# Attention scores whose two matmuls both take 128 rows: each half of q stands twice in SBUF and meets the high and low part of k

## The chip, the cores and the metric

The kernel runs on one core of a Trainium2 chip. The metric is the device time of one execution in microseconds (us). Engines are named as the profile names them: PE is TensorE's matmul stream, PEld its weight loads, DVE VectorE, ACT ScalarE, POOL GpSimd, and SP the engine from whose queue most transfers are issued.

## The reference, cut to what matters

One layer of a bidirectional encoder: a projection, two kinds of attention, an output projection with a LayerNorm, and a mixture of single-neuron experts (PEER). The scores of both attentions are products over a head dimension of 64:

```python
HEAD_DIM = 64
h = x @ w_in[l]                                        # 1024 tokens
# group A: 8 heads, 2 kv heads, blocks of 128 queries against 3 blocks of keys
s = jnp.einsum('bnqkgd,bnskd->bnkgqs', qb, kw).astype(jnp.float32) * (HEAD_DIM ** -0.5)
# group B: 8 heads, a window of 8 rows by 16 columns of the token grid
s = jnp.einsum('brqhd,brikhd->brhqik', qg, kr).astype(jnp.float32) * (HEAD_DIM ** -0.5)
...
x = layer_norm(ALPHA * x + mixed, ln1_g[l], ln1_b[l])
x = layer_norm(ALPHA * x + peer(x, peer_wq[l], peer_keys[l], peer_u[l], peer_v[l]), ln2_g[l], ln2_b[l])
```

## The kernel before

The kernel works in full float32 precision from a narrower matmul type: an operand is split into a high part and a low part (`split`, line 85: ACT rounds, DVE takes the rest), and the product is the sum of high by high, high by low and low by high, in one PSUM accumulation.

The program has three parts. **Projection and first attention** (to about 310 us of the trace): `project(0)` and `project(1)` multiply the input's halves of 512 tokens by 18 column groups of `w_in`, in the order of the table `PORD`. Groups 0 to 7 give q, 8 to 12 give k, 13 to 17 give v. The split q and k go to DRAM tiles `qd` and `kd` through POOL's queue, from two-buffer tiles `sh` (high) and `sl` (low): for each group of q three stores, high, low and high again, so that `qd` holds for each head 64 rows of high, 64 of high once more and 64 of low. For each group of k two stores, high and low. **Attention and routing** (to about 1156 us): for each of 8 blocks of 128 tokens `att_steps(t)` computes group A, then group B. `att_out` follows for each pair of blocks (line 486), then `route`, which picks the experts (lines 558 to 565, `top16` and `decode` on DVE), scatters gate values from POOL (line 165), and `build`, which writes dense gate matrices for three blocks (lines 605 to 620). **Experts** (to the end): the dense half on PE (`hstage`, `vres`, `vflush`) with gathers on POOL and DVE beside it.

The order of the instructions on each engine is made by the framework's scheduler, which interleaves these steps by its own model of their durations; each engine then takes its instructions strictly in that order.

A score is made in `scores` (line 381): `kk` holds a head's keys, 64 rows of high and 64 of low. The first matmul has as weights `qq`, 128 rows (high q twice), and meets all of `kk`. The second has `ql`, 64 rows (low q), and meets the high 64 rows of `kk` alone. Both write one PSUM tile `ps` (two buffers). DVE then adds the bias, takes the row maximum and moves the score to SBUF in one instruction (lines 408 for A, 455 for B). There are 24 such pairs in a block of tokens, 192 in all, of 256, 288 or 384 columns. `load_q` fetches `qq` and `ql` for four heads with one transfer each from SP's queue, 32 times.

Of the kernel before, what the change touches and what calls it, by code (L numbers as in the profile page):

```python
# [11 lines left out]
F32 = mybir.dt.float32  # L12
F32R = mybir.dt.float32r
# [8 lines left out]
P = 128  # L22
S = 1024
# [34 lines left out]
def trunk(ctx, tc, x, xt, wqk, wo, gn, sink, biasa, biasb, ln, wq, keyst, uv, ut, vt, out):  # L58
    nc = tc.nc
    f = lambda ap: ap.bitcast(F32)  # L60
# [24 lines left out]
    def split(hi, lo, raw, lo_eng=None):  # L85
        cp = nc.scalar.copy(hi, raw)  # L86
        nc.vector.tensor_sub(lo, raw, f(hi))  # L87
        return cp

    def mm3(ps, wh, wl, mh, ml, first, last):  # L90
        nc.tensor.matmul(ps, wh, mh, start=first, stop=False)  # L91
        nc.tensor.matmul(ps, wh, ml, start=False, stop=False)  # L92
        nc.tensor.matmul(ps, wl, mh, start=False, stop=last)  # L93
# [10 lines left out]
        nc.vector.scalar_tensor_tensor(tmp, r, mv[:, 0:1], lnt[:, 0, :], op0=OP.subtract, op1=OP.mult)  # L104
        nc.vector.scalar_tensor_tensor(dst, tmp, rs[:, 0:1], lnt[:, 1, :], op0=OP.mult, op1=OP.add)

    qd = tc.dram_tile([16, 3, 64, S], F32, name="qd")
    kd = tc.dram_tile([10, 2, 64, S], F32, name="kd")
    xs = tc.dram_tile([NT, P, D], F32, name="xs")
    wqd = tc.dram_tile([16, 2, P, KT, P], F32, name="wqd")  # L110
# [129 lines left out]
    with ExitStack() as att:  # L240
# [3 lines left out]
        qp = att.enter_context(tc.tile_pool(name="qp", bufs=2))  # L244
# [18 lines left out]
        def load_w(src):  # L263
            raw = wp.tile([P, KT, P], F32, name="wraw", bufs=WB)
            nc.sync.dma_start(raw, src)
            hi = wp.tile([P, KT, P], F32R, name="whi", bufs=WB)
            lo = wp.tile([P, KT, P], F32R, name="wlo", bufs=WB)
            split(hi, lo, raw)
            return hi, lo

        def project(half):
            o = half * 512
            ts = slice(4 * half, 4 * half + 4)
            xs_ = []
            first = load_w(wqk[PORD[0]])
            for k in range(KT):
                raw = wp.tile([P, 512], F32, name="xraw", bufs=5)
                (nc.scalar if half == 0 and k % 2 else nc.sync).dma_start(raw, xt[:, k, o:o + 512])
                xh = xp.tile([P, 512], F32R, name=f"xh{k}")
                xl = xp.tile([P, 512], F32R, name=f"xl{k}")  # L280
                split(xh, xl, raw)
                xs_.append((xh, xl))
            for n, c in enumerate(PORD):
                hi, lo = first if n == 0 else load_w(wqk[c])
                ps = pp.tile([P, 512], F32, name="pq", bufs=2)
                for k, (xh, xl) in enumerate(xs_):
                    mm3(ps, hi[:, k, :], lo[:, k, :], xh, xl, k == 0, k == KT - 1)
                if c < 13:
                    sh = wp.tile([P, 512], F32R, name="sh")
                    sl = wp.tile([P, 512], F32R, name="sl")  # L290
                    if c < 8:
                        sc = wp.tile([P, 512], F32, name="qo")
                        nc.scalar.activation(sc, ps, AF.Copy, scale=0.125)
                    else:
                        sc = ps
                    last = split(sh, sl, sc)
                    for i, m in ((0, sh), (2 if c < 8 else 1, sl)):
                        if c < 4:
                            g0 = 4 * (c // 2) + c % 2
                            dst = qd[g0:g0 + 3:2, i, :, o:o + 512]  # L300
                        elif c < 8:
                            dst = qd[2 * c:2 * c + 2, i, :, o:o + 512]
                        else:
                            dst = kd[2 * (c - 8):2 * (c - 8) + 2, i, :, o:o + 512]
                        nc.gpsimd.dma_start(dst, f(m))
                    if c < 8:
                        nc.gpsimd.dma_start(qd[g0:g0 + 3:2, 1, :, o:o + 512] if c < 4 else qd[2 * c:2 * c + 2, 1, :, o:o + 512], f(sh))
                else:
                    va = wp.tile([P, 512], F32, name="qo")
                    last = nc.scalar.copy(va, ps)  # L310
                    pt = pp.tile([P, 4, P], F32, name="pv")
                    for j in range(4):
                        nc.tensor.transpose(pt[:, j, :], va[:, j * P:(j + 1) * P], ident)
                    nc.vector.tensor_copy(v[:, ts, (c - 13) * P:(c - 12) * P], pt)
# [50 lines left out]
        def att_steps(t):  # L365
            tok = slice(t * P, (t + 1) * P)

            def load_q(grp):
                qq = qp.tile([P, 4, P], F32R, name="qq")
                ql = qp.tile([64, 4, P], F32R, name="ql")  # L370
                grp = qd[4 * grp:4 * grp + 4, :, :, tok].rearrange("h i p n -> (i p) h n")
                nc.sync.dma_start(f(qq), grp[0:P])
                nc.sync.dma_start(f(ql), grp[P:])
                return qq, ql

            def load_k(hd, k0, n):
                kk = kp.tile([P, 576], F32R, name="kk")
                nc.sync.dma_start(f(kk[:, :n]), kd[hd, :, :, k0:k0 + n].rearrange("i p n -> (i p) n"))
                return kk

            def scores(ps, q, i, kk, cols):
                qq, ql = q
                nc.tensor.matmul(ps, qq[:, i, :], kk[:, cols], start=True, stop=False)
                nc.tensor.matmul(ps, ql[:, i, :], kk[0:64, cols], start=False, stop=True)

            blocks = [m for m in (t - 1, t, t + 1) if 0 <= m < NT]
            n = P * len(blocks)
# [8 lines left out]
            for hb in range(2):  # L396
                ss = {}
                q = load_q(hb)
                for i in (2 * hb, 2 * hb + 1):
                    for g in range(2):  # L400
                        ps = ps_s.tile([P, 512], F32, name="ps")
                        scores(ps[:, :n], q, 2 * g + i - 2 * hb, ka[g], slice(0, n))
                        h = 4 * g + i
# [11 lines left out]
                sl = lambda a: hv(a)[:, :, i0:i0 + 2]  # L415
# [13 lines left out]
            if t < 2 or t > 5:  # L429
                n, hw, k0 = 512, 256, 0 if t < 2 else 512  # L430
            else:
                n, hw, k0 = 576, 288, (t - 2) * P
# [5 lines left out]
            for hb in range(2):  # L438
                h0 = 4 * hb
                heads = list(range(h0, h0 + 4))  # L440
                ss = {}
                q = load_q(2 + hb)
                for i in (2 * hb, 2 * hb + 1):
                    for e in range(2):
                        h = 2 * i + e
                        kk = load_k(2 + h, k0, n)
                        bt = bp.tile([P, 576], F32, name="bt")
                        nc.sync.dma_start(bt, biasb[t, h])
                        s = sp.tile([P, 576], F32, name="s")
                        ss[h] = s  # L450
                        for j in range(2):
                            js = slice(j * hw, (j + 1) * hw)
                            ps = ps_s.tile([P, 512], F32, name="ps")
                            scores(ps[:, :hw], q, h - h0, kk, js)
                            nc.vector.tensor_tensor_reduce(s[:, js], ps[:, :hw], bt[:, js], 1.0,
                                                           mx2[:, h:h + 1] if j else BIG, OP.add, OP.max,
                                                           (mx if j else mx2)[:, h:h + 1])
                nc.vector.tensor_scalar_mul(negm[:, h0:h0 + 4], mx[:, h0:h0 + 4], -1.0)
                for h in heads:
                    last = softmax(ss[h], n, negm, den, h)  # L460
                clear(last, ZA[t] if t < len(ZA) else 0)
                nc.vector.reciprocal(den[:, h0:h0 + 4], den[:, h0:h0 + 4])
                attend(y, heads, ss, n, k0 // P, None,
                       [[(h % 2, P + 64 * h, h - h0, h // 2) for h in (h0 + 2 * i, h0 + 2 * i + 1)] for i in range(2)])
# [37 lines left out]
        def att_main(t):  # L502
            for _ in steps[t]:
                pass

        project(0)
        load_ln(0)
        att_head(0)
        att_main(0)
        att_head(1)  # L510
        att_main(1)
        att_out(0)
        project(1)
        pj.close()
        rs = late.enter_context(tc.tile_pool(name="rs", bufs=2, side="right", reuse_waits="tile"))
# [271 lines left out]
    for c in range(ND):  # L787
        if c < RES:
            r = gp.tile([P, 2 * D], F32, name="uv")[:, 0:D]
            nc.scalar.dma_start(r, xs[c])  # L790
            nc.vector.scalar_tensor_tensor(r, r, ALPHA, po[c].rearrange("p j c -> p (j c)"), op0=OP.mult, op1=OP.add)
        else:
            r = facc[c - RES].rearrange("p j c -> p (j c)")
# [72 lines left out]
```

## Time and profile before

| | before |
|---|---|
| median of 3 runs | 3006.41 us (3004.22 to 3008.86) |
| the profiled execution's own time | 3008.4 us |
| its span in the profile | 3006.6 us |
| PE busy | 2803.2 us (93%) |
| DVE busy | 2412.6 us (80%) |
| ACT busy | 1201.7 us (40%) |
| POOL busy | 1085.2 us (36%) |
| mean DMA traffic | 284 GB/s |

The span is the time between the first and the last instruction on the core; the execution's own time has 1.8 us around it. A busy PE includes the time in which a matmul's tail runs beside the next one, so the share of the span says little about how dense the stream is; the starts of neighbouring instructions say more.

### The profile page before, as it was taken

The page shows a single profiled execution, that of the slowest core. Times are in us where ns is not written, and L with a number is a line of the kernel's source. Part 1 is how long each engine was busy: PE and PEld are TensorE (multiplying, and loading weights), DVE is VectorE, ACT ScalarE, POOL GpSimd, SP SyncE. Part 2 cuts the span into 40 slices and gives each one's busy share as a digit, 9 for nine tenths or more (in the row PEclk, how much of TensorE's full clock was granted, in tenths as well). Part 3 has the DMA queues.
Part 4 walks back from the last instruction along what each step waited for, and adds up shares of the span by engine and source line. Part 5 has one row for each costly group of instructions (what it writes and reads, how often), then busy time and mean ns, then how long its engine had stood idle before and what let it go on. Part 6 is the DMA issues. An engine that isn't in the chain of part 4 may idle for free.

```text
span 3006.6 us, 43280 instructions
## 1 busy us (share of the span) xinstructions
PE 2803.2 (93%) x15569; PEld 2379.3 (79%) x15569; DVE 2412.6 (80%) x5427; ACT 1201.7 (40%) x2486; POOL 1085.2 (36%) x748
## 2 busy tenths in 40 slices
PE   6998899998998785999999999999999999999997
PEld 5766567575785775898898889989889899889885
DVE  3343267887988978898998998999999889989975
ACT  2344155242686672333333333333333333333332
POOL 1211001078888881233333333333333333333310
PEclk8999989799899797999999999999999999999998
DMA  7798588796887675998999989999999899899861
GB/s 239 214 269 264 188 298 284 239 268 153 243 231 227 176 212 201 337 341 317 335 343 331 333 328 343 335 346 330 332 342 346 292 352 339 323 339 359 325 245 49
DMA packets 384119, 854.43 MB, mean 284 GB/s; under 512 B 90016, under 2 KB 241568, under 8 KB 332960
## 3 DMA queue, kind: packets, MB, share of 16 engines
q0 software_dynamic: 132672, 437.68, 42.0%
q1 hardware_dynamic: 221600, 384.62, 37.6%
q10 hardware_dynamic: 29632, 29.37, 3.3%
q8 instruction: 122, 2.00, 0.3%
q14 instruction: 93, 0.76, 0.1%
HBM read 761.01 MB, written 90.31 MB: 283 GB/s over the span
## 4 chain that ended last, share of the span: by engine, by line
PE 72%; DMA 11%; DVE 9%; ACT 5%; issue 3%; POOL 1%; SPq 0%; ACTq 0%; DVEq 0%; POOLq 0%
PE h L91 9%; PE h L92 9%; PE h L93 9%; PE po L739 5%; PE po L740 5%; PE po L741 5%; PE fl L739 3%; PE fl L740 3%; PE fl L741 3%; PE ps L486 3%; PE y L362 2%; PE pq L558 2%; PE pr L618 2%; DMA gd<-stage 1%; PE pq L559 1%
## 5 line engine op out<-in xcount | busy, mean ns | idle before, releaser
L659 POOL DMA_INDIRECT uv<-in_uv_dram,eidx x384 | 572.6, 1491 | 1184.8 <-DVE acc L671 755.7
L91 PE MATMUL h<-dh,uh 128*128 128x320 f32 x2048 | 639.9, 312 | 45.1 <-ACT gl L721 22.5
L93 PE MATMUL h<-dh,ul 128*128 128x320 f32 x2048 | 634.6, 310 | 0.4 <-DVE ul L87 0.4
L92 PE MATMUL h<-dl,uh 128*128 128x320 f32 x2048 | 634.1, 310 | 0.0
L165 POOL DMA_INDIRECT gs<-gated,idxd x256 | 440.3, 1720 | 169.0 <-DMA qlo<-wqd 86.7
L661 DVE SCALAR_TENSOR_TENSOR uv<-uv,xg 128x1024 f32<-128x1024 f32 x384 | 467.0, 1219 | 41.9 <-DMA uv<-in_uv_dram,eidx 41.8
L671 DVE SCALAR_TENSOR_TENSOR acc<-uv,hh,acc 128x1024 f32<-128x1024 f32 x381 | 487.7, 1280 | 3.7
L91 PEld LDWEIGHTS h<-dh,uh 128*128 128x128 f32 x2048 | 386.1, 189 | 76.4 <-ACT gl L721 43.8
L92 PEld LDWEIGHTS h<-dl,uh 128*128 128x128 f32 x2048 | 386.2, 189 | 11.4
L93 PEld LDWEIGHTS h<-dh,ul 128*128 128x128 f32 x2048 | 386.1, 189 | 3.3 <-DVE ul L87 0.8
L739 PE MATMUL po<-vh,ah 128*128 128x512 f32 x768 | 288.4, 391 | 0.5 <-ACT ah L86 0.5
L740 PE MATMUL po<-vl,ah 128*128 128x512 f32 x768 | 287.6, 390 | 0.0
L741 PE MATMUL po<-vh,al 128*128 128x512 f32 x768 | 260.9, 391 | 0.0
L767 ACT COPY fl<-fl 128x512 f32<-128x512 f32 x252 | 147.1, 584 | 277.2 <-PE fl L741 276.8
L665 ACT ACTIVATE hh<-hh 128x1 f32<-128x1 f32 x384 | 77.6, 202 | 435.4 <-DVE uv L661 434.2
L721 ACT ACTIVATE gl<-h 128x320 f32<-128x320 f32 x256 | 111.5, 436 | 284.0 <-PE h L93 282.2
L768 DVE TENSOR_TENSOR facc<-facc,fl 128x512 f32<-128x512 f32 x252 | 173.1, 687 | 63.8 <-ACT fl L767 62.8
L739 PE MATMUL fl<-vh,ah 128*128 128x512 f32 x512 | 202.2, 395 | 6.5 <-ACT fl L767 4.3
L740 PE MATMUL fl<-vl,ah 128*128 128x512 f32 x512 | 202.1, 395 | 0.0
L741 PE MATMUL fl<-vh,al 128*128 128x512 f32 x512 | 200.0, 391 | 0.0
L87 DVE TENSOR_TENSOR ul<-raw,uh 128x1024 fp32r<-128x1024 f32 x128 | 156.2, 1220 | 49.6 <-ACT uh L86 48.8
L86 ACT CAST uh<-raw 128x1024 fp32r<-128x1024 f32 x128 | 134.2, 1048 | 122.5 <-PE h L92 71.7
(201 smaller groups left out, 5454.0 us busy)
## 6 DMA issues: line engine op xcount, KB each, us to landing
raw<-in_ut_dram SPq DMA_DIRECT2D x128, 512.0 KB
raw<-in_vt_dram SPq DMA_DIRECT2D x128, 512.0 KB
qhi<-wqd SPq DMA_DIRECT2D x48, 512.0 KB
qlo<-wqd SPq DMA_DIRECT2D x48, 512.0 KB
gd<-stage SPq DMA_DIRECT2D x12, 2048.0 KB
gt<-gd SPq DMA_DIRECT2D x32, 768.0 KB
wraw<-in_wqk_dram SPq DMA_DIRECT2D x36, 512.0 KB
bt<-in_biasb_dram SPq DMA_DIRECT2D x64, 288.0 KB
```

The lines of the kernel that those rows point to most:

```text
L87: nc.vector.tensor_sub(lo, raw, f(hi))
L91: nc.tensor.matmul(ps, wh, mh, start=first, stop=False)
L92: nc.tensor.matmul(ps, wh, ml, start=False, stop=False)
L93: nc.tensor.matmul(ps, wl, mh, start=False, stop=last)
L165: st = nc.gpsimd.indirect_dma_start(out=gs, out_offset=bass.IndirectOffsetOnAxis(ap=idx[:, k:k + 1], axis=0), in_=g[:, k:k + 1], in_offset ...
L659: nc.gpsimd.indirect_dma_start(out=u, out_offset=None, in_=uv, in_offset=bass.IndirectOffsetOnAxis(ap=eidx[t][:, k:k + 1], axis=0))
L661: nc.vector.scalar_tensor_tensor(u[:, 0:D], u[:, 0:D], 1.0, x1[t], op0=OP.mult, op1=OP.mult, accum_out=hh[:, k:k + 1])
L671: nc.vector.scalar_tensor_tensor(acc, u[:, D:], hh[:, k:k + 1], acc, op0=OP.mult, op1=OP.add)
L739: nc.tensor.matmul(ps, ah[:, cs], vh[:, js], start=first, stop=False)
L740: nc.tensor.matmul(ps, ah[:, cs], vl[:, js], start=False, stop=False)
L741: nc.tensor.matmul(ps, al[:, cs], vh[:, js], start=False, stop=last)
L768: nc.vector.tensor_add(acc[:, j, :], acc[:, j, :], fl)
```

## The change

The DRAM tile `qd` keeps two parts per head, high and low, each stored once. `load_q` fetches one tile `qq` of 128 rows by two parts: each part is loaded twice, to rows 0 to 63 and to rows 64 to 127, in four transfers of 64 rows. In `scores` the first matmul is high q (twice) against high and low k as before, and the second is low q (twice) against high and low k, with 128 rows where it had 64. The product of low q and low k, which was left out, is now added.

```diff
-    qd = tc.dram_tile([16, 3, 64, S], F32, name="qd")
+    qd = tc.dram_tile([16, 2, 64, S], F32, name="qd")
...
-                    for i, m in ((0, sh), (2 if c < 8 else 1, sl)):
+                    for i, m in enumerate((sh, sl)):
...
-                    if c < 8:
-                        nc.gpsimd.dma_start(qd[g0:g0 + 3:2, 1, :, o:o + 512] if c < 4 else qd[2 * c:2 * c + 2, 1, :, o:o + 512], f(sh))
...
-                qq = qp.tile([P, 4, P], F32R, name="qq")
-                ql = qp.tile([64, 4, P], F32R, name="ql")
-                grp = qd[4 * grp:4 * grp + 4, :, :, tok].rearrange("h i p n -> (i p) h n")
-                nc.sync.dma_start(f(qq), grp[0:P])
-                nc.sync.dma_start(f(ql), grp[P:])
-                return qq, ql
+                qq = qp.tile([P, 2, 4, P], F32R, name="qq")
+                src = qd[4 * grp:4 * grp + 4, :, :, tok].rearrange("h i p n -> i p h n")
+                for i in range(2):
+                    for r in range(2):
+                        nc.sync.dma_start(f(qq[64 * r:64 * r + 64, i]), src[i])
+                return qq
...
-                qq, ql = q
-                nc.tensor.matmul(ps, qq[:, i, :], kk[:, cols], start=True, stop=False)
-                nc.tensor.matmul(ps, ql[:, i, :], kk[0:64, cols], start=False, stop=True)
+                nc.tensor.matmul(ps, q[:, 0, i, :], kk[:, cols], start=True, stop=False)
+                nc.tensor.matmul(ps, q[:, 1, i, :], kk[:, cols], start=False, stop=True)
```

The scheduler makes a new order of the whole program from this. On PE, in the first projection, this is the difference where the first score stands; rows with `pq` are the projection's matmuls, 24 to a column group, of which only the last two of one group are shown, and `pv` are v's transposes:

```order
 L92 MATMUL pq<-xl_219,whi 128x512
 L93 MATMUL pq<-xh_218,wlo 128x512
+L380 MATMUL ps<-kk,qq 128x256 x2
...
-L383 MATMUL ps<-kk,qq 128x256
-L384 MATMUL ps<-kk,ql 128x256
-L313 MATMUL pv<-ident,qo 128x128 x4
+L381 MATMUL ps<-kk,qq 128x256
+L311 MATMUL pv<-ident,qo 128x128 x4
```

The first score matmul now stands one column group (24 matmuls) earlier, with that of a second head right behind it, and the second halves come after that group.

On SP's queue, in the same stretch, the loads of q before the change stand so among those of the projection's weights (`wraw`) and of the bias (`bt`):

```order
L265 DMA wraw<-in_wqk_dram 128x1024 x2
L372 DMA qq<-qd 128x4x128
L373 DMA ql<-qd 64x4x128
L265 DMA wraw<-in_wqk_dram 128x1024
L372 DMA qq<-qd 128x4x128
L265 DMA wraw<-in_wqk_dram 128x1024
L373 DMA ql<-qd 64x4x128
L405 DMA bt<-in_biasa_dram 128x256
```

And after it:

```order
L265 DMA wraw<-in_wqk_dram 128x1024
L371 DMA qq<-qd 64x4x128
L265 DMA wraw<-in_wqk_dram 128x1024
L371 DMA qq<-qd 64x4x128 x3
L265 DMA wraw<-in_wqk_dram 128x1024
L371 DMA qq<-qd 64x4x128 x3
L265 DMA wraw<-in_wqk_dram 128x1024
L371 DMA qq<-qd 64x4x128
L402 DMA bt<-in_biasa_dram 128x256
```

Two sets of two loads have become two sets of four, and the first of them stands one load of weights earlier.

## Rows read from the trace of the kernel before

**Rows 1.** The page's head: span and number of instructions.

```profile
span 3006.6 us, 43280 instructions
```

**Rows 2.** Stretches: length, then busy us (instructions) by engine, clock, DMA share, GB/s.

```profile
0.00:310.00 310.00, 264.29 (x1179) 198.25 (x1180) 115.25 (x256) 111.61 (x192) 55.26 (x76) 0.94 0.83 246
310.00:765.00 455.00, 418.37 (x2288) 286.20 (x2287) 314.55 (x1395) 165.51 (x356) 145.19 (x112) 0.91 0.78 240
...
940.00:1156.00 216.00, 151.69 (x939) 134.09 (x939) 191.31 (x820) 136.77 (x323) 163.97 (x89) 0.82 0.72 211
1156.00:3006.00 1850.00, 1800.28 (x9984) 1621.48 (x9984) 1646.30 (x2417) 651.60 (x1292) 572.62 (x384) 0.99 0.86 316
```

**Rows 3.** The score's two matmuls by line: ns min/median/max, first and last start, forms.

```profile
L383 PE MATMUL ps<-kk,qq x192: 275/384/690, 63.0 to 894.5; 128*128 128x256 f32 x80, 128*128 128x288 f32 x64, 128*128 128x384 f32 x48
L384 PE MATMUL ps<-kk,ql x192: 379/394/687, 70.8 to 894.9; 64*128 64x256 f32 x80, 64*128 64x288 f32 x64, 64*128 64x384 f32 x48
```

**Rows 4.** Timeline of PE at 407 and 410 us: start, duration, instruction, weights' rows*columns.

```profile
406.89 0.28 PE L559 MATMUL pq<-tl,qhi 128*128 128x256 f32 x1
407.01 0.28 PE L560 MATMUL pq<-th,qlo 128*128 128x256 f32 x1
407.13 0.29 PE L383 MATMUL ps<-kk,qq 128*128 128x288 f32 x1
407.35 0.40 PE L384 MATMUL ps<-kk,ql 64*128 64x288 f32 x1
407.68 1.16 PE L333 MATMUL pt<-rb,ones 128*128 128x128 f32 x8
...
410.56 0.40 PE L384 MATMUL ps<-kk,ql 64*128 64x288 f32 x1
410.89 0.40 PE L383 MATMUL ps<-kk,qq 128*128 128x288 f32 x1
411.22 0.39 PE L384 MATMUL ps<-kk,ql 64*128 64x288 f32 x1
411.54 0.71 PE L565 MATMUL pq<-kt,q 128*128 128x128 f32 x4
```

**Rows 5.** Timeline of the weight loads at 418 us; idle time before in brackets.

```profile
418.60 0.20 PEld L362 LDWEIGHTS y<-pT,v 128*64 128x64 f32 x4
418.96 0.20 PEld L362 LDWEIGHTS y<-pT,v 64*64 64x64 f32 x4 [0.17 <-issue]
419.33 0.85 PEld L362 LDWEIGHTS y<-pT,v 128*64 128x64 f32 x16 [0.17 <-issue]
```

**Rows 6.** Chain of waits from 310 to 765 us, shares by line.

```profile
by line: PE ps L486 15.1%; PE y L362 8.1%; DMA wo<-in_wo_dram 7.1%; PE pq L558 6.8%; PE pt L351 6.2%; PE pq L560 5.7%; PE pq L559 5.7%; PE ps L384 5.0%; issue 4.1%; PE ps L383 3.5%; PE pq L565 2.9%; DVE s L408 1.9%; DVE big L203 1.3%; DVE t
```

**Rows 7.** The score's evacuation on DVE, to 920 us: busy us, mean ns, idle before.

```profile
L455 DVE CUSTOM_DVE_ANT_0 s<-ps,bt,mx 128x256 f32<-128x256 f32 (+1 forms) x64 | 31.6, 494 | 20.8 <-PE ps L384 18.7 <-PE pt L333 1.1
```

**Rows 8.** The loads of q on SP's queue: ns min/median/max of the issue.

```profile
L372 SPq DMA_DIRECT2D qq<-qd x32: 370/384/3066, 53.6 to 841.9; - x32
L373 SPq DMA_DIRECT2D ql<-qd x32: 585/586/2484, 56.1 to 842.3; - x32
```

**Rows 9.** Who waited for q's stores, to 920 us: us, times, longest.

```profile
DVE sl L87 <- DMA qd<-sl: 54.4, 9, 12.1
...
ACT sh L86 <- DMA qd<-sh: 39.2, 9, 11.1
```

**Rows 10.** PE's waits from 50 to 100 us: us, times, longest.

```profile
PE ps L384 <- DMA ql<-qd: 7.2, 1, 7.2
PE ps L383 <- DMA qq<-qd: 5.5, 1, 5.5
```

**Rows 11.** What SP's loads of k waited for, 310 to 765 us.

```profile
SPq L378 <- PE ps L384: 35.1, 26, 4.2
```

**Rows 12.** Chain of waits from 765 to 1156 us, shares by line.

```profile
by line: PE pr L618 12.1%; DMA gd<-stage 11.3%; ACT stage L619 10.1%; PE pq L558 5.1%; ACT qj L614 4.9%; PE pq L559 4.3%; PE pq L560 4.3%; issue 4.1%; DVE pi L605 3.3%; DVE qj L609 3.3%; PE ps L486 2.6%; PE y L362 2.5%; DVE t L126 1.8%; PE 
```

**Rows 13.** DMA issues: the stores of high q.

```profile
qd<-sh POOLq DMA_DIRECT2D x32, 256.0 KB
```

## The prediction, made before the changed kernel ran

> **What bounds the kernel now.** I read the stretches of the program first [rows 2]. They cut the span of 3006.6 us [rows 1] into a projection stage to 310 us, attention with routing to 1156 us and the experts after it. The expert stage is PE's: 1800 of 1850 us busy. It holds no score, so the change can only move its beginning, apart from a shuffled order inside it. From 310 to 765 us PE is busy for 418 of 455 us and DVE for 315; the chain of waits there lies mostly on PE's lines [rows 6]. From 940 to 1156 us PE has 152 of 216 us and DVE 191, and the chain from 765 us on is one of building the gate matrices, with ACT, DVE and a store taking turns [rows 12]. So time saved on PE counts most between 310 and 765 us.
>
> Then the timeline of PE, which shows what a score costs. Two neighbouring matmuls of 256 columns with full 128 by 128 weights start 0.12 us apart (406.89, 407.01, 407.13) [rows 4]. The score's second matmul, with 64 rows, starts 0.33 us after the first (410.89 to 411.22), and the next instruction of full rows again 0.33 us after it (407.35 to 407.68, 411.22 to 411.54, and 410.56 to 410.89 where the next score follows). It is not the score's operands that do this: where the values' matmuls go from 128 rows to 64 and back, the weight loads stand idle for 0.17 us each time, for nothing that the profile shows [rows 5], and inside a run of one shape they don't. I read it as the price of changing the number of rows: a following load is not taken ahead of the running matmul.
>
> **The change part by part.** *The matmuls.* At the pace of the 128-row stream 288 columns would take 0.12 x 288/256 = 0.135 us. A change of rows thus costs 0.33 - 0.135 = 0.195 us, a pair has two, so 0.39 us, and 192 pairs [rows 3] at most 75 us of PE. Less where the weights were ready and the second half came after 0.22 us (407.13 to 407.35), and less where the next matmul has 64 columns of weights, since there the shape changes anyway. Less too where scores follow each other at once: DVE empties a chunk in 0.494 us [rows 7] from two buffers, so such a pair goes from 0.66 us to no less than 0.49. The doubled rows themselves cost nothing by the rows: the medians of the two matmuls are 384 and 394 ns, the one with half the rows the longer [rows 3].
>
> What of this lies on the path, by stage:
>
> 310 to 765 us: the chain spends 5.0% + 3.5% of 455 us on the two score lines, 38.7 us [rows 6]. Of each, 0.195/0.33 = 59% goes: 23 us. Bounds 0 and 23. I take three quarters, 17 us, since DVE at 315 of 455 us and the waits for the output weights (7.1%) come next and do not shrink.
>
> 765 to 1156 us: the score lines stand behind the last shown share, 1.8%, so under 7 us each [rows 12]; 59% of 14 is 8, and I take half, 4 us.
>
> 0 to 310 us: two blocks, 48 pairs, 19 us of PE, in a stage where PE already stands for 46 us [rows 2]. I take a third, 6 us.
>
> *The stores.* 16 stores of 256 KB [rows 13] leave POOL's queue; with 8 groups of q and 5 of k in two halves, 48 + 20 stores become 32 + 20, or 24% fewer. ACT and DVE wait 39.2 and 54.4 us to reuse the two `sh` and `sl` buffers until a store has landed [rows 9]. A quarter of that is 22 us, the upper bound; the lower is nothing, as other transfers fill the freed time. I take 4 us: these waits lie in the stage with a DMA share of 0.83, and PE is covered through most of them.
>
> *The loads.* Four issues of the 64-row form at 0.586 us replace one of 0.384 and one of 0.586 [rows 8]: 2.34 - 0.97 = 1.37 us more of SP per set, 44 us over 32 sets, and 512 KB for 384 a set. What hides it: SP's queue mostly waits for PE to release a buffer, as in the loads of k, 35.1 us for the score's second matmul alone [rows 11], and PE waits for q only once, at the very first score [rows 10]. There it stands for 5.5 + 7.2 us. The new order puts the first score 24 matmuls of 512 columns earlier, by the pace above 24 x 0.24 = 5.8 us of work that no longer covers the wait. Queued behind it on PE is the whole projection. Bounds: a loss of 5.8 us, or none if the stores land earlier; I take 5.
>
> [...]
>
> The sum: 17 + 4 + 6 + 4 - 5 = 26 us. The profiled execution took 3008.4 us, so 2982.4; it lies 2.0 us over the median of the runs shown, and for a median I forecast 2980 us. If everything on the upper side came true, 23 + 8 + 19 + 22 = 72 us, it would be 2934.
>
> **The rivals.** *Absorbed.* PE's freed time turns into waits for DVE, for the output weights or in the gate building, and the expert stage begins hardly sooner. For it: DVE at 69% between 310 and 765 us and 89% after 940 [rows 2]; the chain there hardly touches a score. Against it: the chain does run through the score lines before 765 us. A quarter of the forecast's gain, 6 us, is left: 3000 us.
>
> *No effect of the rows.* The 0.33 us belongs to something else, say to the second weights being fetched from a tile of their own, and stays. Then only loads and stores change: -4 + 5, about 3007 us. Against it stand the values' loads, which show the same gap at a change of rows and no other [rows 5]. [...]
>
> *Slower: the loads of q.* If SP's 44 us of extra issue come onto the path, because the loads of k and the bias behind them land late and PE, now faster, waits for them, the gain of 26 us is eaten. It decides once more than 26 of the 44 us show, that is when over half the sets (about 19 of 32) stall PE for their 1.37 us; with all, 2980 + 44 = 3024 us. For it: every set is four issues in a row on a queue that takes its work in order. Against it: SP waits for PE, not PE for SP, in all but one place.
>
> **How the numbers follow.** Chances: the forecast and beyond, a gain of 12 us or more, 0.65; absorbed 0.15; no effect 0.07; slower 0.13. The likeliest case has 2950 to 2994 us for itself: at its lower end 56 of the 72 us of upper bounds, at its upper end 12 us. The range takes in the absorbed case and no effect: 2950 to 3008 us, which leaves out the slower case and the last of the bounds. A difference of 0.2%, 6 us, is about what a measurement of this kernel can tell from none. Of the absorbed case half falls over that (0.08), so faster 0.73; the other half (0.07) and no effect (0.07) are the same, 0.14; slower 0.13. A new order in the expert stage may add some us either way; with 50 us of PE idle in it, I give it no sign.
>
> **What the profile after would show.** The second score matmul with 128 rows, starting 0.13 to 0.17 us after the first and followed as closely: this step right. Spacings of 0.33 us still there: wrong. The expert stage beginning at some 1130 us where it is 1156 now: the forecast; near 1150 with more PE waits for DVE: absorbed. PE or DVE waits for loads of q, k or bias that grow by 20 us or more: the slower case. First score's wait at 13 us or more: the early loss. Waits for q's stores falling from 94 us by a quarter: the stores. The forecast is wrong if the time between 310 and 765 us shrinks by under 8 us though the pairs are tight.

## The result and the profile after

The changed kernel takes 2980.94 us (median of 4 runs, 2980.01 to 2985.32), the kernel before 3005.31 us beside it (4 runs, 2998.56 to 3008.86). The ratio is 0.9933, 95% interval 0.991 to 0.9956: faster by 24 us. The profiled execution took 2985.32 us.

The head of the page of the changed kernel, with the busy time of each engine:

```profile
span 2981.6 us, 43327 instructions
...
PE 2733.9 (92%) x15569; PEld 2357.3 (79%) x15569; DVE 2408.1 (81%) x5427; ACT 1202.3 (40%) x2486; POOL 1065.1 (36%) x732
```

The span shrank by 25.0 us [rows 1], PE's busy time by 69.3 us from 2803.2. So PE was freed of nearly all of the 75 us that the prediction gave as the most, and a third of it reached the end.

PE's timeline at 395 us, where the blocks' scores stand (start, duration, instruction, weights' rows*columns):

```profile
395.46 0.38 PE L380 MATMUL ps<-kk,qq 128*128 128x288 f32 x1
395.67 0.29 PE L381 MATMUL ps<-kk,qq 128*128 128x288 f32 x1
395.80 0.29 PE L380 MATMUL ps<-kk,qq 128*128 128x288 f32 x1
395.93 0.29 PE L381 MATMUL ps<-kk,qq 128*128 128x288 f32 x1
396.06 0.60 PE L562 MATMUL pq<-kt,q 128*128 128x128 f32 x4
396.75 0.40 PE L380 MATMUL ps<-kk,qq 128*128 128x288 f32 x1
396.99 0.29 PE L381 MATMUL ps<-kk,qq 128*128 128x288 f32 x1
397.13 0.39 PE L555 MATMUL pq<-th,qhi 128*128 128x256 f32 x1
```

Inside the run from 395.67 to 396.06 each matmul starts 0.13 us after the one before, where 0.33 us stood [rows 4]. At the beginning of a run (395.46, 396.75) the second half still comes 0.21 to 0.24 us after the first. The two matmuls and their second weight load, by line (ns min/median/max, first and last start):

```profile
L380 PE MATMUL ps<-kk,qq x192: 278/378/690, 66.3 to 860.6; 128*128 128x256 f32 x80, 128*128 128x288 f32 x64, 128*128 128x384 f32 x48
...
L381 PEld LDWEIGHTS ps<-kk,qq x192: 187/191/338, 74.1 to 860.6; 128*128 128x128 f32 x192
L381 PE MATMUL ps<-kk,qq x192: 275/294/526, 74.4 to 860.7; 128*128 128x256 f32 x80, 128*128 128x288 f32 x64, 128*128 128x384 f32 x48
```

The second matmul's median fell from 394 to 294 ns [rows 3] though it has twice the rows, and the last score begins at 860.7 us instead of 894.9.

The stretches of the program (length, then busy us and instructions of PE, PEld, DVE, ACT, POOL, clock, DMA share, GB/s):

```profile
310.00:765.00 455.00, 397.15 (x2391) 290.60 (x2390) 328.54 (x1453) 174.03 (x370) 154.47 (x117) 0.91 0.82 251
...
1131.00:2981.00 1850.00, 1799.97 (x9984) 1619.04 (x9984) 1641.07 (x2401) 652.84 (x1292) 570.43 (x384) 0.99 0.86 317
```

Against [rows 2], the 455 us from 310 us on hold 103 more PE instructions with 21 us less of busy time. PE's idle time there has grown from 37 to 58 us. What PE waits for in it (total us, times, longest):

```profile
PE ps L380 <- DVE mx L405: 10.7, 9, 2.5
PE ps L483 <- DMA wo<-in_wo_dram: 10.7, 5, 6.2
PE pt L349 <- ACT s L315: 9.6, 15, 2.6
PE pq L555 <- ACT sc L564: 6.4, 6, 2.9
```

Before, in the same stretch:

```profile
PE ps L486 <- DMA wo<-in_wo_dram: 14.7, 8, 6.3
PE ps L383 <- DVE mx L408: 4.7, 9, 1.0
PE pt L351 <- ACT s L317: 3.3, 6, 1.1
```

The waits for DVE's row maximum and for ACT's softmax have grown by 6 us each: part of PE's freed time has turned into waiting for the engines that empty its results.

The expert stage takes 1850 us as before, with the same 9984 matmuls. It begins earlier: its first matmul stands at 1133.34 us after the change (1156.85 before):

```profile
1133.34 0.64 PE L91 MATMUL h<-dh,uh 128*128 128x320 f32 x1 [25.65 <-ACT uh L86]
```

What lets it begin is read off the chain that ended last, in order of time, just ahead of it (start, us, piece):

```profile
1112.73 1.55 POOL gs L165
...
1114.59 4.18 DMA gs<-gated,idxd
...
1119.07 0.37 SPq L700
...
1124.24 7.67 DMA raw<-in_ut_dram
```

POOL's last scatter of gate values (line 165) lands, SP then loads the gates (`gt<-gs` and `gt<-gd`, lines 700 and 705), and the first expert weights `raw` stand behind these on SP's queue. Two chains must end before that load: POOL's 256 scatters, one behind the other, and the building of the dense gate matrices with its 12 stores (`gd<-stage`). Before, the second ended last. Both, by line, in the kernel before (ns min/median/max, first and last start), and SP's first loads of gates behind them:

```profile
L165 POOL DMA_INDIRECT gs<-gated,idxd x256: 1543/1547/5056, 608.3 to 1128.7; - x128
...
L620 SPq DMA_DIRECT2D gd<-stage x12: 319/320/423, 815.4 to 1135.5; - x12
...
1142.00 0.37 SPq L703 DMA_DIRECT2D gt<-gs  x1
```

And in the changed kernel:

```profile
L165 POOL DMA_INDIRECT gs<-gated,idxd x256: 1543/1547/5346, 597.5 to 1114.6; - x128
...
L617 SPq DMA_DIRECT2D gd<-stage x12: 319/320/424, 801.5 to 1109.1; - x12
...
1119.07 0.37 SPq L700 DMA_DIRECT2D gt<-gs  x1
```

The last store moved up by 26.4 us, the last scatter by 14.1 us, the gates' load by 22.9 us: 3.5 us of what the building gained went to waiting for the scatters. From the gates' load to the end it is 1864.6 us before and 1862.5 us after. These are milestones of one execution of each kernel; how far such milestones can be trusted is shown below the table of the experiments.

### The profile page after: what moved, and what is told of

It is laid out like the page before. It is cut to its first block, busy times and chain, and to the rows that moved or that the text cites. A ratio compares the mean times of both kernels' runs of the same rounds, so it can differ in the third digit from the quotient of the medians.

```text
span 2981.6 us, 43327 instructions
## 1 busy us (share of the span) xinstructions
PE 2733.9 (92%) x15569; PEld 2357.3 (79%) x15569; DVE 2408.1 (81%) x5427; ACT 1202.3 (40%) x2486; POOL 1065.1 (36%) x732
## 4 chain that ended last, share of the span: by engine, by line
PE 48%; DVE 5%; DMA 4%; issue 3%; ACT 2%; POOL 1%; SPq 0%; ACTq 0%; POOLq 0%; DVEq 0%
PE h L91 9%; PE h L92 8%; PE h L93 8%; PE po L736 5%; PE po L737 5%; PE po L738 5%; PE fl L737 3%; PE fl L736 3%; PE fl L738 3%; DMA uv<-in_uv_dram,eidx 2%; DMA raw<-in_ut_dram 2%; DVE uv L658 1%; DVE acc L668 1%; POOL uv L656 1%; DVE vl L87 1%
```

## The experiments

The theory after the result: the change of rows on PE gave the gain, and it arrives through the start of the scatters, the end of the building and with them the gates' load. Three rivals were left: the fewer stores and other loads of q did it; a new order of the same work did it; PE still bounds the stages before the experts, so that more would come of still less work. All twelve experiments stand in one table. "Load" is SP's first load of gates in the profiled execution, "to end" the time from there to the end of the span. The milestones and the span belong to that one execution; the median and the ratio (95% interval, to executions of the kernel before that ran beside the experiment) belong to all executions of a kernel.

| kernel | last score | last scatter | last store | load | to end | span | median | ratio to before |
|---|---|---|---|---|---|---|---|---|
| before | 894.9 | 1128.7 | 1135.5 | 1142.0 | 1864.6 | 3006.6 | 3005.31 | |
| after | 860.7 | 1114.6 | 1109.1 | 1119.1 | 1862.5 | 2981.6 | 2980.94 | 0.9933 (0.991 to 0.9956) |
| E1 rows alone | 886.8 | 1138.4 | 1111.4 | 1141.7 | 1870.9 | 3012.6 | 3025.01 | 1.0073 (1.0056 to 1.009) |
| E2 loads and stores alone | 892.3 | 1129.3 | 1130.5 | 1137.4 | 1870.6 | 3008.0 | 3003.77 | 1.0 (0.9986 to 1.0015) |
| E3 after, two tiles | 860.3 | 1114.8 | 1112.2 | 1119.7 | 1860.6 | 2980.3 | 2982.06 | 0.9922 (0.9902 to 0.9941) |
| E7 before, other order | 905.7 | 1115.2 | 1151.4 | 1157.8 | 1870.6 | 3028.4 | 3015.55 | 1.005 (1.0031 to 1.0068) |
| E4 no second matmul | 852.6 | 1108.1 | 1092.6 | 1111.4 | 1864.0 | 2975.4 | 2985.25 | 0.9947 (0.9926 to 0.9968) |
| E5 second matmul twice | 882.1 | 1109.6 | 1106.3 | 1114.9 | 1881.9 | 2996.8 | 2993.17 | 0.9957 (0.9937 to 0.9977) |
| E8 = E1, weights first | 882.6 | 1138.5 | 1107.0 | 1141.7 | 1874.6 | 3016.3 | 3018.32 | 1.0049 (1.0024 to 1.0073) |
| E9 = after, weights first | 857.4 | 1109.7 | 1104.1 | 1115.9 | 1866.1 | 2982.0 | 2978.25 | 0.9914 (0.9893 to 0.9936) |
| E6 both matmuls 64 rows | 877.5 | 1111.7 | 1112.8 | 1119.7 | 1868.2 | 2987.8 | 2989.59 | one run |
| E10 = E1, half the scatters | 895.3 | 877.4 | 1116.9 | 1123.3 | 1880.5 | 3003.8 | 2997.06 | 0.997 (0.9955 to 0.9985) |
| E11 = before, half the scatters | 885.4 | 857.0 | 1119.6 | 1126.0 | 1862.5 | 2988.5 | 3003.44 | 0.9986 (0.9969 to 1.0002) |
| E12 = after, half the scatters | 849.4 | 839.5 | 1096.7 | 1103.2 | 1869.9 | 2973.1 | 2976.47 | 0.9901 (0.9874 to 0.9927) |

The profiled execution can lie far from the median: E1's is 10.5 us under it, E7's 15 us over it, E11's 13 us under it. And some kernels have the same order of PE, SP and POOL up to the first scatter, so that their milestones can be compared. That scatter starts at 597.5, 595.6 and 586.3 us in the changed kernel, E9 and E12, at 608.3 and 603.1 us in before and E11, and at 610.5, 607.0 and 620.0 us in E1, E8 and E10. A shift of one milestone by up to 13 us is therefore no effect by itself. The scatters of E8 and E10, by line:

```profile
L165 POOL DMA_INDIRECT gs<-gated,idxd x256: 1543/1547/5165, 607.0 to 1138.5; - x128
...
L165 POOL DMA_INDIRECT gs<-gated,idxd x128: 1543/1547/3007, 620.0 to 877.4; - x128
```

### The parts of the change by themselves

**E1: the rows alone.** The stores of before, and low q loaded twice:

```diff
-                ql = qp.tile([64, 4, P], F32R, name="ql")
+                ql = qp.tile([P, 4, P], F32R, name="ql")
-                nc.sync.dma_start(f(ql), grp[P:])
+                nc.sync.dma_start(f(ql[0:64]), grp[P:])
+                nc.sync.dma_start(f(ql[64:P]), grp[P:])
...
-                nc.tensor.matmul(ps, ql[:, i, :], kk[0:64, cols], start=False, stop=True)
+                nc.tensor.matmul(ps, ql[:, i, :], kk[:, cols], start=False, stop=True)
```

> The kernel before with the matmul part of the change alone: low q is loaded to both halves of the rows (three loads per set) and the second matmul takes 128 rows; the three stores per group of q stay. If the change of rows was the price (my theory), nearly the whole gain is here: 17 + 4 + 6 us less, about 2980 us, and the spacing of the second half to the next matmul falls from 0.33 to 0.135 us for 288 columns. If the dropped stores made the gain, the time stays near 3005 us. If the new order of instructions made it, the time can be anywhere between 2985 and 3015 us, since this kernel has an order of its own.

Measured: 3025.01 us, 0.7% slower than before; this expectation fell. Yet the building of the gates did end earlier: its last store stands at 1111.4 us, within 3 us of the changed kernel's. What came last instead are the scatters, 10 us later than before, and in E8, which has the same order up to the experts, at the same place (1138.5 us). By line, and on SP's timeline:

```profile
L165 POOL DMA_INDIRECT gs<-gated,idxd x256: 1542/1547/5172, 610.5 to 1138.4; - x128
...
1111.37 0.32 SPq L621 DMA_DIRECT2D gd<-stage  x1
...
1141.69 0.37 SPq L704 DMA_DIRECT2D gt<-gs  x1
```

The load of gates stands 30 us behind the last store, where before it stood 6.5 us behind it, and thus where it was before. The span is even 6 us longer than before, all of it after the gates' load; and the profiled execution is the fastest of the six, so the median's loss of 22 us is seen only in part. The scatters thus explain why the load gained nothing; why E1 is slower than before is not shown.

**E2: the loads and stores alone.** The changed kernel with the second matmul back at 64 rows:

```diff
-                nc.tensor.matmul(ps, q[:, 1, i, :], kk[:, cols], start=False, stop=True)
+                nc.tensor.matmul(ps, q[0:64, 1, i, :], kk[0:64, cols], start=False, stop=True)
```

> The changed kernel with its two stores per group and four loads per set, but the second matmul with 64 rows as before. My theory: the spacings of 0.33 us are back and the time is 3000 to 3010 us, within 5 us of the kernel before. If stores or loads made the gain: 2975 to 2985 us. If the order made it: anywhere between.

Measured: 3003.77 us against 3002.86, ratio 1.0 (0.9986 to 1.0015). The second matmul's median is back at 393 ns, as expected. Fewer stores and more issues of loads come to nothing, together. With the changed kernel's loads and stores, the change of rows is then worth 3003.77 - 2982.06 (E3, on the same chip) = 22 us, in the orders that these kernels got.

**E3: the changed kernel with its two halves of q in two tiles.** The same work in another order:

```diff
-                qq = qp.tile([P, 2, 4, P], F32R, name="qq")
+                qq = [qp.tile([P, 4, P], F32R, name=n) for n in ("qq", "ql")]
...
```

> The changed kernel with high and low q in two tiles in place of one: the same matmuls, stores and loads, but the scheduler gives the program another order. It measures what an order alone is worth. My theory: within 6 us of the changed kernel, 2975 to 2987 us. If the gain of 24 us is the luck of an order, it can come out near 3000 us.

**E7: the kernel before with the two loads of q exchanged.** Again the same work in another order:

```diff
-                nc.sync.dma_start(f(qq), grp[0:P])
                 nc.sync.dma_start(f(ql), grp[P:])
+                nc.sync.dma_start(f(qq), grp[0:P])
```

> The kernel before with the two loads of a set issued the other way round, low q first: the same work, but another order of the program. Together with the two-tile kernel it gives the size of the order's noise. My theory: 2999 to 3012 us. If the gain is the luck of an order: it can come out near 2985 us.

E3 gave the changed kernel's time (2982.06 us). E7 gave 3015.55 us, 12.7 us over before, outside what was expected; in its profiled execution, 15 us over the median, the building ends 16 us later. So an order alone can move this kernel by more than 10 us, and a difference of that size between two kernels here is not a cause by itself. For the change of rows it says that two orders with it lie at 2981 and 2982, and three without it (before, E2, E7) at 3003 to 3016; E1 and its variant E8 break this row. What holds in all orders with every scatter is the end of the building: with 128 rows in both matmuls its last store stands at 1104 to 1112 us (after, E1, E3, E8, E9), with 64 rows in the second at 1130 to 1151 us (before, E2, E7), one execution each. With half of the scatters the same comparison (E10 and E12 against E11) gives 1116.9 and 1096.7 against 1119.6 us, which does not show it for E10.

### Is it PE?

**E4: the second matmul left out.**

```diff
-                nc.tensor.matmul(ps, q[:, 0, i, :], kk[:, cols], start=True, stop=False)
-                nc.tensor.matmul(ps, q[:, 1, i, :], kk[:, cols], start=False, stop=True)
+                nc.tensor.matmul(ps, q[:, 0, i, :], kk[:, cols], start=True, stop=True)
```

> The changed kernel without the score's second matmul at all (low q is loaded but not used, so that part of each score is left out). It takes some 0.135 to 0.2 us of PE per pair away, 26 to 38 us in all, without any change of rows. If PE were still what ends the attention part, 10 us or more would come off (2970 us or less). My theory is that the chain of scatters on POOL now ends last there, and that it starts when DVE has decoded the first two blocks: 2974 to 2986 us, and the experts still begin when the scatters are done. An order of its own adds some 5 us either way.

**E5: the second matmul done twice**, with 128 rows each time:

```diff
+                nc.tensor.matmul(ps, q[:, 1, i, :], kk[:, cols], start=False, stop=False)
                 nc.tensor.matmul(ps, q[:, 1, i, :], kk[:, cols], start=False, stop=True)
```

> The changed kernel with the second matmul done twice (the low part of q counts double), all with 128 rows: 192 matmuls more, 26 to 38 us of PE, no change of rows. If PE's time in the attention part still reaches the end by half, as I took it for the time freed: 12 to 20 us more, 2993 to 3001 us. If it is off the path: 2981 us. If a third matmul costs as much as the change of rows did (some 75 us of PE): back at 3003 us or more.

E4's median of 2985.25 us is no better than the changed kernel's, and within what its theory said. Of the 26 to 38 us of PE's time that were expected to go, 17 went (2716.6 us busy). In the profiled execution, the fastest of its six, the building ends 16.5 us earlier (1092.6), but the load only 7.7 us, because it waits for the scatters (1108.1).

E5 took 2993.17 us, 12 us over the changed kernel by the medians and 7 us by the ratios, whose intervals overlap; PE is busy for 20 us more (2754.1 us). This time lies at the edge of the range named for the case that PE's time still reaches the end by half. The milestones do not show it in that way: the last score comes 21 us later, but the load of gates no later than in the changed kernel (1114.9 against 1119.1); the loss lies in "to end", 1881.9 us. Of these 19 us, 8 are busy time of PE for the same 9984 matmuls (1808.2 against 1800.0 us), the rest is waiting. What causes it is open. In these two executions, then, the score's matmuls did not set when the experts began; E5's time does not rule out that PE still counts.

### The price of a change of rows

**E6: both matmuls with 64 rows.**

```diff
-                nc.tensor.matmul(ps, q[:, 0, i, :], kk[:, cols], start=True, stop=False)
-                nc.tensor.matmul(ps, q[:, 1, i, :], kk[:, cols], start=False, stop=True)
+                nc.tensor.matmul(ps, q[0:64, 0, i, :], kk[0:64, cols], start=True, stop=False)
+                nc.tensor.matmul(ps, q[0:64, 1, i, :], kk[0:64, cols], start=False, stop=True)
```

> The changed kernel with both matmuls of a score on 64 rows (high q by high k and low q by high k; high q by low k is left out). One look, for the spacings. If the price belongs to a change of the number of rows: between the two halves of a score 0.12 to 0.22 us, as with 128 rows in both, and 0.3 us or more between the second half and a next matmul of 128 rows. If it belongs to weights of 64 rows as such: 0.3 us or more also between the two halves.

PE's timeline of E6 around a lone pair, and around two pairs that follow each other:

```profile
394.88 0.28 PE L557 MATMUL pq<-th,qlo 128*128 128x256 f32 x1
395.09 0.40 PE L380 MATMUL ps<-kk,qq 64*128 64x288 f32 x1
395.33 0.29 PE L381 MATMUL ps<-kk,qq 64*128 64x288 f32 x1
395.55 1.16 PE L331 MATMUL pt<-rb,ones 128*128 128x128 f32 x8
...
398.30 0.40 PE L380 MATMUL ps<-kk,qq 64*128 64x288 f32 x1
398.54 0.29 PE L381 MATMUL ps<-kk,qq 64*128 64x288 f32 x1
398.66 0.35 PE L380 MATMUL ps<-kk,qq 64*128 64x288 f32 x1
398.86 0.29 PE L381 MATMUL ps<-kk,qq 64*128 64x288 f32 x1
399.08 0.71 PE L562 MATMUL pq<-kt,q 128*128 128x128 f32 x4
```

In these rows neighbours that both have 64 rows stand 0.12 to 0.24 us apart, about as expected for a price of the change. The other half of the expectation fell: the full matmul behind a pair follows after 0.22 us, not 0.3 or more. So the 0.33 us of before belongs neither to 64 rows as such nor to the score's operands, and a single change does not always show as 0.33 us. What holds is the total. From the last full matmul ahead of a lone pair to the first behind it are 395.55 - 394.88 = 0.67 us here, and 407.68 - 407.01 = 0.67 us before [rows 4], with two changes in either; at the unbroken pace it is 0.12 + 2 x 0.135 = 0.39. The changed kernel shows this pace around a lone pair, 400.36 - 399.98 = 0.38 us:

```profile
399.98 0.28 PE L557 MATMUL pq<-th,qlo 128*128 128x256 f32 x1
400.10 0.29 PE L380 MATMUL ps<-kk,qq 128*128 128x288 f32 x1
400.23 0.29 PE L381 MATMUL ps<-kk,qq 128*128 128x288 f32 x1
400.36 0.83 PE L331 MATMUL pt<-rb,ones 128*128 128x128 f32 x6
```

A change thus costs 0.14 us around a lone pair, and 0.195 us where each matmul has another number of rows than its neighbours.

### What holds the gates' load

**E8 and E9: the first expert weights loaded ahead of the gates**, in E1 and in the changed kernel:

```diff
+        if e == 0:
+            rawv = dn.tile([P, D], F32, name="raw", bufs=3)
+            nc.sync.dma_start(rawv, vt[0:P, :])
+            load_g(0)
+            load_g(1)
...
-    load_g(0)
     for e in range(ne):
...
```

> The kernel with the matmul part alone (first experiment) plus one edit at the beginning of the experts: the first loads of expert weights stand ahead of the loads of the gates on SP's queue. The order on PE is the same as there up to the experts. There the experts' first matmul stood at 1156 us although the gate building had ended at 1110, and SP waited 29.5 us for the scatters with the weight loads queued behind. If that wait is why the matmul part alone came out slow: the first matmul at 1125 to 1140 us and 10 to 20 us less than 3025. If the slowness lies in the order before or in the experts: the first matmul moves, the end does not, 3020 to 3030 us.

> The changed kernel with the same edit: expert weights ahead of the gates on SP's queue, the order on PE the same up to the experts. SP waited 9 us for the scatters there. Theory: the experts' first matmul moves from 1133 to about 1125 us and 4 to 9 us come off, 2972 to 2977 us. Rival: the memory of the first weights is released no earlier, or the gates are needed at once anyway: 2981 us.

Here the theory was that the gates matter only because the weights queue behind them on SP. In E8's profiled execution it fell: the weights load at 1113.69 us and the experts' first matmul starts at 1119.0, 37 us before E1's, but the load of gates stands where it was, and so does the end:

```profile
1113.69 0.33 SPq L713 DMA_DIRECT2D raw<-in_ut_dram  x1
...
1141.70 0.38 SPq L704 DMA_DIRECT2D gt<-gs  x1
...
L91 PE MATMUL h<-dh,uh x2048: 302/309/635, 1119.0 to 2981.4; 128*128 128x320 f32 x187
```

E1's row for the same line, for comparison:

```profile
L91 PE MATMUL h<-dh,uh x2048: 302/309/633, 1155.8 to 2978.5; 128*128 128x320 f32 x187
```

The last of these matmuls starts at 2981.4 us, not before E1's 2978.5: in these two executions what counts is when the gates are there. By the medians E8 lies 7 us under E1, between the two ranges that were named for it, and the intervals of the two ratios overlap. E9's first expert matmul starts at 1116.1 us, 17 us before the changed kernel's, and its median is 2.7 us under the changed kernel's, likewise between its ranges, which these runs do not tell from none.

**E10, E11, E12: half of the scatters**, in E1, in before and in the changed kernel; half of the gate values of the first two blocks are left out:

```diff
-            for h in range(8):
+            for h in range(4):
...
-            for b in added[t, 7]:
+            for b in added[t, 3]:
```

> The kernel with the matmul part alone, with the scatters of 4 heads out of 8 (half of the gate values of the first two blocks are left out; the order on PE is all but the same). There the first load of the gates stood at 1141.7 us, behind the last scatter at 1138.4, while the gate building had ended at 1111. If the chain of scatters is what ate the gain: that load at about 1118 us, and some 23 us less than 3025: 2998 to 3005 us. If the slowness lies elsewhere: 3020 us or more.

> The kernel before with half of the scatters left out, the order on PE the same. There the gates' load waited for the last store of the gate building (1135.5 us, load at 1142.0), not for the scatters (1128.7). Theory: no gain, the load at 1138 to 1142 us and 3000 to 3006 us. If the scatters held up the kernel before too, by what POOL takes from DVE or by DMA traffic: 10 us or more less.

> The changed kernel with half of the scatters left out, the order on PE the same. There scatters (last at 1114.6 us) and gate building (last store at 1109.1) end nearly together, the gates' load is at 1119.1 us. Theory: the load moves to 1115 us, by the building's last store, and 2 to 6 us come off: 2975 to 2979 us. If the scatters hid more of the matmuls' gain: 10 us or more come off, 2971 us or less.

E10 is 28 us under E1, a little more than expected, with the load 6.5 us behind the last store again:

```profile
1116.86 0.32 SPq L621 DMA_DIRECT2D gd<-stage  x1
...
1123.33 0.37 SPq L704 DMA_DIRECT2D gt<-gs  x1
```

The kernel before gains nothing that can be measured from the same omission (E11, 0.9986 with 1 in its interval), as expected, though the one execution that was profiled, the second fastest of its 12, has its load 16 us earlier. The changed kernel's median falls by 4.5 us (E12), as expected, which its interval does not tell from none; its load comes 16 us earlier, but the way from there to the end is 7 us longer. A part of these two shifts was there before the missing scatters could act: the first scatter already stands 5 us earlier in E11 and 11 us earlier in E12. Of the medians, E1's alone moves clearly, and there the scatters came last by 27 us.

E10's fair partner is E11, which leaves out the same scatters. Against it the rows alone gain 6 us (2997.06 and 3003.44; the intervals of the ratios overlap), while the whole change gains 27 us (E12). So without half of the scatters E1's loss is gone, but the gain of the change is not back: 21 us remain between E10 and E12, which differ by the stores and loads of q and by the order.

## Why the prediction was right, and where its steps were not

The forecast of 2980 us lies 1 us from the median, inside 2950 to 2994, the likeliest case's own range. The total owes something to terms that erred in opposite directions, and the parts that were tried by themselves (E1, E2) do not add up to it: that it was met so closely is in part luck.

**The price of the rows: right.** 0.33 us became 0.13 us, the second matmul's median fell by 100 ns, and PE lost 69 of at most 75 us. The doubled rows cost PE nothing that shows. "No effect of the rows" is refuted as far as PE and the building go: with 128 rows in both matmuls PE is busy for 2734 to 2737 us (after, E1, E3, E8, E9), with 64 in the second for 2800 to 2808 us (before, E2, E7), and the building's last store lies at least 18 us apart. For the kernel's time it is shown only together with the new stores and loads, where E2 and E3 lie 22 us apart, in one order without the rows and two with them; E1, which has the rows and the old stores, is slower than before. The weight loads show the same difference. In the kernel before, the load of 128 rows behind full rows at 407.01 us starts together with the matmul ahead of its own, which follows at 407.13; the loads of 64 rows at 407.35, 410.56 and 411.21 us start within 0.01 us of their own matmuls [rows 4]:

```profile
407.01 0.19 PEld L383 LDWEIGHTS ps<-kk,qq 128*128 128x128 f32 x1
407.35 0.18 PEld L384 LDWEIGHTS ps<-kk,ql 64*128 64x128 f32 x1
...
410.56 0.18 PEld L384 LDWEIGHTS ps<-kk,ql 64*128 64x128 f32 x1
410.89 0.19 PEld L383 LDWEIGHTS ps<-kk,qq 128*128 128x128 f32 x1
411.21 0.18 PEld L384 LDWEIGHTS ps<-kk,ql 64*128 64x128 f32 x1
```

In the changed kernel, with all 128 rows on both sides, loads of 0.19 us go with starts 0.13 us apart. Two next matmuls there with 64 columns of weights start 0.22 us after the second half (643.84 to 644.06 and 646.15 to 646.37 us), where those with 128 columns shown above start after 0.13 to 0.14.

**The stages: the sizes were off.** The milestones by which the gain can be followed, of the two profiled executions: the first store of the routing's q (`wqd`) moved from 354.6 to 349.3 us, so 5.3 us came up to there (forecast: 6 + 4 - 5 = 5). The first matmul of the building moved from 783.8 to 772.0: 6.5 us more, where the term for 310 to 765 us was 17. The last store moved by 26.4: 14.6 us more, where the term for 765 to 1156 us was 4. The load gave 3.5 us back to the scatters, and the span behind it gained 2.1: 5.3 + 6.5 + 14.6 - 3.5 + 2.1 = 25.0. The surest of these is the 6.5: from `wqd` to the building's first matmul are 429.2 us before and 428.9 in E11, which has the same order, against 422.7, 422.0 and 422.8 in the changed kernel, E9 and E12. The stretch ahead of it is the least sure: `wqd` stands at 354.6 and 348.7 us in the one order, at 349.3, 347.1 and 338.2 in the other. The step that failed is "I take three quarters, 17 us": the freed PE time of that stretch went into longer waits for DVE and ACT (+12 us in the two groups shown of both kernels) and into work that the new order pulled forward: the building stretch was then shorter by 62 PE instructions (2018 to 1956 between its first matmul and its last store) and by 24 us of PE time. By its own test, a shrinkage of under 8 us between 310 and 765 us, the prediction named itself wrong; that test was badly put, since the order does not keep work inside a stretch.

**The chain behind it: not named.** The prediction had the building's stores before the experts and left out the scatters, the last of which started only 7 us before the last store (1128.7 against 1135.5). In the changed kernel's profiled execution they hold the load; E1 and E8 show that they can eat what the building gained, E10 that with half of them E1's loss goes, but not that the gain comes back. "Absorbed" was the nearest rival, with another mechanism: 44 of PE's 69 us did not reach the end; new waits and a chain that is not PE's stand where they went.

**The stores: right in time, wrong in size of the waits.** The waits for q's stores should have fallen by a quarter. They fell from 93.6 to 14.5 us [rows 9], while those for k's stores beside them grew from 16.0 to 21.9 us. DVE's and ACT's waits up to 920 us:

```profile
DVE sl L87 <- DMA kd<-sl: 13.6, 5, 7.4
DVE sl L87 <- DMA qd<-sl: 10.5, 4, 6.2
...
ACT sh L86 <- DMA qd<-sh: 4.0, 1, 4.0
```

It is the stores that do it: 88.0 us of these waits remain in E1, which has the stores of before, 7.7 us in E2, which has the new ones. Yet E2 is no faster than before (0.9986 to 1.0015), so by themselves these waits cost the end nothing that shows, and the two terms' sum of 4 - 5 = -1 us was good for stores and loads together as far as E2 goes; the two are not tested apart.

**The loads of q: right.** The first score waits 12.6 us in one piece, where it waited 5.5 + 7.2 in two [rows 10]; the loss from its earlier place is at most the 3.3 us by which it stands later (63.0 to 66.3). Elsewhere PE waits for q 0.6 us in all up to 920 us. The rival of SP's extra issues is refuted by this and by E2. The issue on SP is dearer for the 64-row form here (0.586 against 0.384 us [rows 8]); in E2 four of them a set, with fewer stores, cost no time that shows.

**What stays open.** Why POOL's chain of scatters is 528 us long in E1's order (531.5 in E8) where the changed kernel's is 517; that its first scatter comes at 610.5 instead of 597.5 is within what one order shows. Why E5's and E10's experts take some 18 us more from the gates' load on. And how much of the 24 us is the order's luck: the two parts of the change do not add, as the rows alone gave +22 us, the loads and stores alone 0, both together -24. It may be that the waits for stores matter once PE is fast, though E1's building ends no later than the changed kernel's, or that E1's order is a bad one; only one order of it was run, besides E8's edit of its loads, and orders of the same work differ by 10 us and more.

## What to carry to other kernels

Where a matmul of fewer rows stands between full ones, look at the distance of the starts, not at the durations: here each change between 64 and 128 rows cost 0.14 to 0.2 us, as much as the matmul itself at the unbroken pace (0.135 us), and filling the idle rows, with keys that lay in SBUF anyway and low q loaded a second time, cost no time that shows: the second matmul's median went from 394 to 294 ns, and E2, with the loads, lies at 1.0 of before (0.9986 to 1.0015). Before pricing time that PE is to be freed of, list every chain that must end before the next stage begins, with its end; the gain can end at the second of them, which here had its last piece only 7 us ahead of the first. Where a scheduler remakes the order for each edit, reorder the same work once or twice, and profile the same order more than once, before giving a cause to 10 us. And when a load is lightened to see what it hides, lighten it in the kernel before too: E10 alone looked like the gain coming back, E11 beside it shows that most of it had not.

## What the runs showed that was not expected

A lone pair with 64 rows in both halves and one with 128 and 64 cost PE the same 0.67 us between their full neighbours (E6 and before), though the rows change at different places. Sixteen stores of 256 KB fewer, out of 68, took 85% of the waits for q's buffers away (93.6 to 14.5 us), and no time that E2 tells from none. And exchanging two load instructions of one function, with all work unchanged, moved the kernel by 12.7 us (E7).
